# RWKV-7 mixer: a chunk's last doubling joins the first doubling of the next visit, and the products with the state take the array's full shape

## The chip, the cores and the metric

The kernel runs on one core of one Trainium2 chip. The metric is device time in microseconds of one execution, taken as the median of several runs. Beside them stands one execution under the hardware profiler, from which all rows below come.

## The reference

Two layers of a trunk over 1024 latent and 256 context tokens of width 1024, all in float32. Each layer: a modulated norm, one input projection, three groups of heads (gated linear attention, GLA; windowed softmax attention; RWKV-7), one output projection, and a SwiGLU feed-forward part. The change lies in the RWKV-7 scan, four heads of width 64 in two directions:

```python
def step(S, inp):
    rt, wt, kt, vt, kkt, at = inp
    sa = jnp.einsum('bhvk,bhk->bhv', S, kkt)
    S = (S * wt[:, :, None, :] - sa[..., None] * (kkt * at)[:, :, None, :]
         + vt[..., None] * kt[:, :, None, :])
    return S, jnp.einsum('bhvk,bhk->bhv', S, rt)
```

The kernel computes it in chunks of 64 tokens. Inside a chunk the sequential updates make a triangular system of 64x64 for each head and direction, so the kernel needs the inverse X of a unit triangular matrix. It finds it by doubling: the inverses of diagonal blocks of 2, 4, 8, 16 and 32 rows one after the other, and last the 64x64 one from its two blocks of 32. One doubling is two products with a copy between them: y = L·X of the smaller blocks, then w = X·y is put off the diagonal.

## The kernel before

The mixers of a layer run as generators, and a small planner (`Weave`) writes the order of TensorE's instructions by hand. It keeps a clock `TE.t` that each product advances by a planned cost, each generator yields the time it wants to wait before its next step, and of those whose time has come the one with the lowest rank goes first: `scan` (0), `prep` (1), `finish_all` (3), and last (9) the dense products of the input projection (`in_rest`, tile `ps_in`, 128x512 or 128x256), which therefore fill the gaps one by one. A generator can also wait for a mark, `yield after(("s", i - 3))`, until the planner has set it. One column of the projection is held back until the scans are done. The order of the other engines' instructions is the scheduler's, with those that go through `FIRST` preferred.

`prep` (line 1183) makes a visit for each of 20 chunks and one more. In visit i the younger chunk i gets its products with itself (`gram`, tile `ps_g`, 64-row shape, masked by VectorE into LQ), a first level on VectorE, and then the older chunk i-1 gets its own `ps_g` (into MP). Two steps follow in which both chunks double together: 64 products `ps_y` of the shape 32x32 (each float32 product is two instructions), ScalarE's copy y, 64 products `ps_w`, then on VectorE a predicated copy into X2 and a transpose into XT2. Chunk i goes through two doublings in visit i and two in visit i+1. At the end of visit i+1 stands the last doubling, of 32 to 64: 16 instructions into `ps_y6`, a copy, 16 into `ps_w6`, and copies into XF[p], which holds the four 32x32 blocks in 64 columns for each of the four matrices. Between them stand four transposes into `ps_kt`. Then the mark `("b", i - 1)` is set.

`scan` (line 1272) waits for that mark and for the scan before. It makes `ps_r` from two groups of eight full-shape products (MP with the values, AK with the state SBD), copies the result into R, multiplies it by X (128 rows, 64 columns, restarting the upper half of `ps_r`), copies that into VU and U, makes the new state with `ps_s`, sets `("s", i)`, and adds LQ·U (again 64 columns) to the lower half of `ps_r` for the output.

In the profile all products carry line 160 and all preferred instructions line 177, so tiles tell them apart; numbers at the end of a tile's name are left out, so `ps_y6` and `ps_w6` appear as `ps_y` and `ps_w` with 16 instructions.

Of the kernel before, what the change touches and what calls it, by code (L numbers as in the profile page):

```python
# [38 lines left out]
P = 128  # L39
# [106 lines left out]
def block_kernel(ctx: ExitStack, tc: tile.TileContext, a):  # L146
# [975 lines left out]
    def rwkv_mixer(l, t_first, pool, fpool, pp, spawn):  # L1122
# [23 lines left out]
        XF = [pool.tile([P, 4, 64], F32, name=f"XF{i}") for i in range(2)]  # L1146
# [36 lines left out]
        def prep():  # L1183
# [3 lines left out]
            for i in range(NC + 1):  # L1187
                yield after(("s", i - 3))
                p = i % 2
                young, old = batch[i] if i < NC else None, batch[i - 1] if i else None  # L1190
# [32 lines left out]
                for step in range(2):  # L1223
                    py = new([P, 2, 4, 32], "ps_y")
# [3 lines left out]
                    y = pool.tile([P, 2, 4, 32], F32, name="y", bufs=2)  # L1228
                    S.copy(y[:, hv], py[:, hv])
                    yield 1000  # L1230
                    pz = new([P, 2, 4, 32], "ps_w")
# [3 lines left out]
                    V.copy_predicated(f3(X2[:, hv]), lev2[:, step, p, hv].rearrange("p h n -> p (h n)"), f3(pz[:, hv]))  # L1235
                    V.transpose(f3(XT2[:, hv]), f3(X2[:, hv]))
                    yield 1200
                if old is None:
                    continue

                X, XT, LQ, xf = X2[:, 1 - p], XT2[:, 1 - p], old["LQ"], XF[p]
                for r in (0, 32, 64, 96):
                    (S.copy if r < 64 else G.tensor_copy)(xf[r:r + 32, :, r % 64:r % 64 + 32], X[r:r + 32])
                ab = [(h, v, d) for v in range(2) for d in range(2) for h in (0, 64)]
                py = new([P, 2, 32], "ps_y6")
                for h, v, d in ab:
                    ra, rb = (h, h + 32) if d == 0 else (h + 32, h)
                    TE.matmul(py[rb:rb + 32, v, :], LQ[ra:ra + 32, 2 * d + v, rb % 64:rb % 64 + 32],
                              XT[ra:ra + 32, 2 * d + v, :])
                y = pool.tile([P, 2, 32], F32, name="y6")  # L1250
                S.copy(y, py)
# [5 lines left out]
                yield 300  # L1257
                pz = new([P, 2, 32], "ps_w6")
                for h, v, d in ab:
                    ra, rb = (h, h + 32) if d == 0 else (h + 32, h)  # L1260
                    TE.matmul(pz[ra:ra + 32, v, :], y[rb:rb + 32, v, :], X[rb:rb + 32, 2 * d + v, :])
                for h in (0, 64):
                    for d in range(2):
                        ra, rb = (h, h + 32) if d == 0 else (h + 32, h)
                        (V.tensor_copy if d == 0 else S.copy)(
                            xf[ra:ra + 32, 2 * d:2 * d + 2, rb % 64:rb % 64 + 32], pz[ra:ra + 32])
                old["X"] = xf
                at["b", i - 1] = TE.t + 900
# [3 lines left out]
        def scan():  # L1272
            V, S, G = FIRST
            for i in range(NC):
# [19 lines left out]
                for u in range(4):  # L1294
                    TE.matmul(pr_[H[0], u, :], X[:, u, :], R[:, u, :], skip_group_check=True)
# [640 lines left out]
```

## Time and profile before

| | us |
|---|---|
| median of 3 runs | 3733.19 (3726.67 to 3733.74) |
| the profiled execution | 3721.78 |
| its span, first to last instruction | 3719.8 |
| TensorE busy, of the span | 3548.3 |
| VectorE, ScalarE, GpSimd busy | 2347.6, 1518.4, 693.1 |
| mean granted TensorE clock | 0.977 of full speed |

A row of the timeline gives the start of a group of like instructions, the time to the end of its last one, engine, line, operation, tiles, shape and count, and in brackets the idle time of the engine before it with what ended it. Products are pipelined: the end of a group overlaps the start of the next, so the time a group costs is read from its start to the start of the group behind it.

### The profile page before, as it was taken

How to read it: one execution, taken by the hardware profiler on the slowest of the kernel's cores; microseconds unless marked ns; L12 is line 12 of the kernel's file. 1: busy time of each engine (PE TensorE's matmuls, PEld its weight loads, DVE VectorE, ACT ScalarE, POOL GpSimd, SP SyncE). 2: the span in 40 equal slices, each digit the busy share in tenths (PEclk: the TensorE clock that was granted, in tenths of full speed). 3: DMA queues.
4: the chain of work that ended last, by engine and by line, in shares of the span. 5: the costliest groups of instructions: out<-in, count | busy, mean ns of one | idle time of the engine just before them, and what ended most of it. 6: DMA issues, size and time to landing. Idle time of an engine off the chain costs nothing. (4 is left out here: it accounts for less than half of the span.)

```text
span 3719.8 us, 76157 instructions
## 1 busy us (share of the span) xinstructions
PE 3548.3 (95%) x30714; PEld 2800.8 (75%) x30714; DVE 2347.6 (63%) x4516; ACT 1518.4 (41%) x3094; POOL 693.1 (19%) x979
## 2 busy tenths in 40 slices
PE   7988899999999999999999998989899999999998
PEld 4766778656788888888788766777777778888787
DVE  4764555556557777746776783455665676666766
ACT  4434543346324333333442543553366143333213
POOL 3122332111333000000341232232211340000002
PEclk8999999999999999999999999999989999999999
DMA  5253343553331333325421234343321332221611
GB/s 184 105 171 102 110 141 95 138 146 91 98 107 60 109 115 110 112 76 195 133 90 59 83 141 141 114 141 105 95 80 47 122 104 87 82 88 57 204 63 63
DMA packets 310768, 405.78 MB, mean 109 GB/s; under 512 B 52880, under 2 KB 210192, under 8 KB 308368
## 3 DMA queue, kind: packets, MB, share of 16 engines
q1 hardware_dynamic: 310416, 400.92, 34.3%
q8 instruction: 242, 3.96, 0.4%
q14 instruction: 110, 0.90, 0.1%
HBM read 290.54 MB, written 105.03 MB: 106 GB/s over the span
## 5 line engine op out<-in xcount | busy, mean ns | idle before, releaser
L160 PE MATMUL ps_in<-h,w_hl 128*128 128x512 f32 (+1 forms) x2928 | 708.1, 382 | 9.3 <-ACT w_hl L412 2.7
L160 PEld LDWEIGHTS ps_in<-h,w_hl 128*128 128x128 f32 x2928 | 486.6, 192 | 135.7 <-issue 52.1
L160 PE MATMUL ps_gu<-f,hl 128*128 128x512 f32 (+1 forms) x2400 | 566.4, 388 | 7.5 <-DVE hl L413 4.2
L160 PE MATMUL ps_d<-g,w_hl 128*128 128x512 f32 (+1 forms) x2688 | 556.2, 368 | 9.1 <-DVE x L1700 6.7
L160 PEld LDWEIGHTS ps_d<-g,w_hl 128*128 128x128 f32 x2688 | 462.9, 189 | 102.8 <-DVE x L1700 11.3
L160 PEld LDWEIGHTS ps_gu<-f,hl 128*128 128x128 f32 x2400 | 441.2, 189 | 102.2 <-DVE hl L413 5.1
L1700 DVE SCALAR_TENSOR_TENSOR x<-ps_d,mods,x 128x512 f32<-128x512 f32 (+1 forms) x448 | 291.0, 684 | 131.3 <-PE ps_d L160 130.7
L160 PE MATMUL ps_gu<-T,hl 128*128 128x512 f32 x1440 | 346.9, 390 | 1.5 <-DVE u L1601 1.5
L160 PEld LDWEIGHTS ps_gu<-T,hl 128*128 128x128 f32 x1440 | 268.8, 188 | 57.6 <-ACT g L412 1.9
L277 POOL TENSOR_TENSOR ada<-ada 128x256 f32<-128x256 f32 x112 | 89.2, 830 | 690.1 <-DMA x<-d_gt 557.2
L365 POOL TENSOR_TENSOR nacc<-nacc,nsq 128x512 f32<-128x512 f32 (+1 forms) x52 | 60.8, 1169 | 759.6 <-ACT nsq L364 744.6
L412 ACT CAST hl<-S 128x512 fp32r<-128x512 f32 x160 | 98.4, 620 | 249.4 <-PE ps_gu L160 155.8
L412 ACT CAST w_hl<-w_raw 128x1024 fp32r<-128x1024 f32 (+1 forms) x100 | 100.9, 1013 | 235.9 <-PE ps_d L160 199.3
L412 ACT CAST hl<-raw 128x512 fp32r<-128x512 f32 x156 | 96.6, 622 | 219.2 <-PE ps_gu L160 196.2
L1044 DVE TENSOR_REDUCE mx<-ps_ss 128x1 f32<-128x640 f32 (+2 forms) x144 | 107.5, 747 | 115.0 <-PE ps_ss L160 114.6
L160 PE MATMUL ps_o<-m,w_hl 128*128 128x512 f32 (+1 forms) x720 | 169.7, 383 | 0.0
L413 DVE TENSOR_TENSOR hl<-S,hl 128x512 fp32r<-128x512 f32 x160 | 110.0, 689 | 64.9 <-ACT hl L412 64.4
L160 PEld LDWEIGHTS ps_o<-m,w_hl 128*128 128x128 f32 x720 | 124.6, 191 | 31.0 <-issue 7.7
L413 DVE TENSOR_TENSOR w_hl<-w_raw,w_hl 128x1024 fp32r<-128x1024 f32 (+1 forms) x100 | 120.3, 1207 | 40.8 <-ACT w_hl L412 40.5
L413 DVE TENSOR_TENSOR pT<-ps_st,pT 128x512 fp32r<-128x512 f32 (+1 forms) x168 | 109.0, 657 | 33.4 <-ACT pT L412 32.9
L160 PEld LDWEIGHTS ps_x<-f,hl 128*128 128x128 f32 x960 | 124.5, 191 | 6.6 <-issue 0.8
L160 PE MATMUL ps_x<-f,hl 128*128 128x256 f32 x960 | 127.1, 283 | 0.0
(354 smaller groups left out, 5937.9 us busy)
## 6 DMA issues: line engine op xcount, KB each, us to landing
w_raw<-in_w_in_dram SPq DMA_DIRECT2D x44, 512.0 KB, 3.7
raw<-in_w_gate_dram SPq DMA_DIRECT2D x44, 512.0 KB, 3.5
raw<-in_w_up_dram SPq DMA_DIRECT2D x44, 512.0 KB, 3.7
x<-d_gt SPq DMA_DIRECT2D x88, 256.0 KB, 3.2
AK<-d_ab SPq DMA_DIRECT2D x80, 256.0 KB, 3.8
w_raw<-in_w_down_dram SPq DMA_DIRECT2D x40, 512.0 KB, 3.6
d_gt<-u SPq DMA_DIRECT2D x68, 256.0 KB, 2.2
d_ab<-W SPq DMA_DIRECT2D x16, 1024.0 KB, 3.9
```

What stands on the lines that cost most here:

```text
L160: return nc.tensor.matmul(out, lhsT, rhs, **kw)
L277: G.tensor_tensor(acc[:, s], acc[:, s], ps_[n % 2], ALU.add)
L365: (G if 0 < o < 5 else V).tensor_tensor(self.acc[g0], self.acc[g0], sq[:, :n], ALU.add)
L412: S.copy(dst[:, 0], src)
L413: V.tensor_tensor(dst[:, 1], src, dst[:, 0].bitcast(F32), ALU.subtract)
L1044: V.tensor_reduce(m_, psf[:, :nk * P], AX.X, ALU.max)
L1700: V.scalar_tensor_tensor(x[:, o, g0:g0 + n], ps[:, :n], mods[:, l, s, 40 + o:41 + o], x[:, o, g0:g0 + n], ALU.mult, ALU.add)
```

## The change

The visits become 22. The step "double both chunks" of a visit first takes, behind its own products, those of the last doubling of the chunk whose second doubling ended in the visit before; X and XT of that chunk are put into a tile XO for it, since X2 is taken over by the next young chunk. The mark "b" of a chunk is set there. XF is widened to 128 columns, with the right half zero, and holds X less the identity, so that X·R is added to R in `ps_r` in place of restarting it; LQ·U takes all 128 columns of LQ, and its upper half is not read. VU has two buffers in place of three.

```diff
-        XF = [pool.tile([P, 4, 64], F32, name=f"XF{i}") for i in range(2)]
+        XF = [pool.tile([P, 4, P], F32, name=f"XF{i}") for i in range(2)]
...
+            ab = [(h, v, d) for v in range(2) for d in range(2) for h in (0, 64)]
+            of = lambda h, d: (h, h + 32) if d == 0 else (h + 32, h)
+            last = None
-            for i in range(NC + 1):
+            for i in range(NC + 2):
                 yield after(("s", i - 3))
...
-                    old["VU"] = VU = pool.tile([P, 512], F32, name="VU", bufs=3)
+                    old["VU"] = VU = pool.tile([P, 512], F32, name="VU", bufs=2)
...
                     for h, LQ in both:
                         for u, rs, cs in blocks:
                             TE.matmul(py[rs, h, u, :], LQ[rs, u, cs], XT2[rs, h, u, :])
+                    if last is not None:
+                        py6, ob = new([P, 2, 32], "ps_y6"), last
+                        for h, v, d in ab:
+                            ra, rb = of(h, d)
+                            TE.matmul(py6[rb:rb + 32, v, :],
+                                      ob["LQ"][ra:ra + 32, 2 * d + v, rb % 64:rb % 64 + 32], XO[ra:ra + 32, 1, 2 * d + v])
+                    if both:
+                        y = pool.tile([P, 2, 4, 32], F32, name="y", bufs=2)
+                        S.copy(y[:, hv], py[:, hv])
+                    if last is not None:
+                        y6 = pool.tile([P, 2, 32], F32, name="y6")
+                        S.copy(y6, py6)
                     yield 1000
...
+                    if last is not None:
+                        pz6 = new([P, 2, 32], "ps_w6")
+                        for h, v, d in ab:
+                            ra, rb = of(h, d)
+                            TE.matmul(pz6[ra:ra + 32, v, :], y6[rb:rb + 32, v, :], XO[rb:rb + 32, 0, 2 * d + v])
...
+                    if last is not None:
+                        for h in (0, 64):
+                            for d in range(2):
+                                ra, rb = of(h, d)
+                                (V.tensor_copy if d == 0 else S.copy)(
+                                    last["X"][ra:ra + 32, 2 * d:2 * d + 2, rb % 64:rb % 64 + 32], pz6[ra:ra + 32])
+                        at["b", i - 2] = TE.t + 1200
+                        last = None
                     yield 1200
...
+                X, xf = X2[:, 1 - p], XF[p]
+                XO = pool.tile([P, 2, 4, 32], F32, name="XO")
+                S.copy(XO[:, 0], X)
+                S.copy(XO[:, 1], XT2[:, 1 - p])
+                last = old
+                old["X"] = xf
                 for r in (0, 32, 64, 96):
-                    (S.copy if r < 64 else G.tensor_copy)(xf[r:r + 32, :, r % 64:r % 64 + 32], X[r:r + 32])
+                    (V if r < 64 else G).tensor_tensor(
+                        xf[r:r + 32, :, r % 64:r % 64 + 32], X[r:r + 32],
+                        eye32[r:r + 32].unsqueeze(1).to_broadcast([32, 4, 32]), ALU.subtract)
...
                 for u in range(4):
-                    TE.matmul(pr_[H[0], u, :], X[:, u, :], R[:, u, :], skip_group_check=True)
+                    TE.matmul(pr_[:, u, :], X[:, u, :], R[:, u, :], start=False, stop=False, skip_group_check=True)
...
                 for u in range(4):
-                    TE.matmul(pr_[H[1], u, :], LQ[:, u, 64:128], U[:, u, :], start=False, stop=(u == 3),
+                    TE.matmul(pr_[:, u, :], LQ[:, u, :], U[:, u, :], start=False, stop=(u == 3),
                               skip_group_check=True)
```

The lines of the old last doubling at the visit's end (its `ps_y6`, copy, a wait of 300, `ps_w6`, copies, the mark) are taken out there; the four transposes into `ps_kt` stay.

## Rows read from the trace of the kernel before

**Rows 1.** The page, part 1: busy us, share of the span, instructions.
```profile
PE 3548.3 (95%) x30714; PEld 2800.8 (75%) x30714; DVE 2347.6 (63%) x4516; ACT 1518.4 (41%) x3094; POOL 693.1 (19%) x979
```
**Rows 2.** TensorE's waits, 275 to 690 us, then 2270 to 2680: us, times, longest.
```profile
PE ps_y L160 <- DVE XT L177: 10.8, 8, 2.7
PE ps_s L160 <- DVE VU L177: 4.9, 5, 1.0
...
PE ps_y L160 <- DVE XT L177: 9.5, 7, 3.5
PE ps_w L160 <- ACT y L177: 9.0, 9, 2.4
PE ps_r L160 <- ACT Rbd L177: 4.1, 5, 1.5
...
PE ps_y L160 <- DVE rw_rs_t L442: 1.8, 1, 1.8
```
**Rows 3.** Timeline of TensorE, one visit of the first layer (columns as told above).
```profile
640.88 1.66 PE L160 MATMUL ps_in<-h,w_hl 128*128 128x512 f32 x6
642.47 0.33 PE L160 MATMUL ps_y<-XT,LQ 32*32 32x32 f32 x16
642.73 0.66 PE L164 MATMUL ps_kt<-cst,Ke 128*128 128x128 f32 x4
643.14 0.71 PE L160 MATMUL ps_in<-h,w_hl 128*128 128x512 f32 x2
643.78 0.33 PE L160 MATMUL ps_w<-X,y 32*32 32x32 f32 x16
644.04 1.96 PE L160 MATMUL ps_g<-AK 64*64 64x128 f32 x32
...
646.73 1.05 PE L160 MATMUL ps_r<-Vbd,MP 128*128 128x128 f32 x8
647.62 1.06 PE L160 MATMUL ps_r<-SBD,AK 128*128 128x128 f32 x8
648.43 0.71 PE L160 MATMUL ps_in<-h,w_hl 128*128 128x512 f32 x2
...
654.68 1.09 PE L160 MATMUL ps_r<-Ubd,LQ 128*64 128x128 f32 x8
655.70 0.50 PE L160 MATMUL ps_in<-h,w_hl 128*128 128x512 f32 x1
```
**Rows 4.** Timeline of TensorE, the ends of both stretches.
```profile
687.32 7.89 PE L160 MATMUL ps_in<-h,w_hl 128*128 128x512 f32 x35
...
707.85 1.64 PE L160 MATMUL ps_in<-h,w_hl 128*128 128x512 f32 x6
...
2653.41 1.42 PE L160 MATMUL ps_in<-h,w_hl 128*128 128x512 f32 x5
...
2662.53 1.06 PE L160 MATMUL ps_r<-Rbd,XF 128*64 128x128 f32 x8 [0.62 <-ACT Rbd L177]
2663.52 0.45 PE L160 MATMUL ps_w<-X,y 32*32 32x32 f32 x32
2663.90 0.44 PE L164 MATMUL ps_f<-cst,fy 128*128 128x128 f32 x2
...
2673.49 1.06 PE L160 MATMUL ps_r<-Rbd,XF 128*64 128x128 f32 x8 [1.51 <-ACT Rbd L177]
2675.38 1.16 PE L160 MATMUL ps_s<-VU,KT 128*128 128x128 f32 x8 [0.83 <-DVE VU L177]
```
**Rows 5.** By tile: count, shortest/median/longest ns, first and last start in us, forms.
```profile
L160 PEld LDWEIGHTS ps_r<-SBD,AK x320: 192/192/333, 296.5 to 2671.4; 128*128 128x128 f32 x160
L160 PEld LDWEIGHTS ps_r<-Rbd,XF x320: 132/137/137, 299.7 to 2674.2; 128*64 128x64 f32 x160
L177 DVE TENSOR_TENSOR SBD<-ps_s,tmp x80: 374/422/429, 304.8 to 2677.1; 64x256 f32<-64x256 f32 x80
```
**Rows 6.** Timeline of TensorE at the longest wait for XT in the first layer.
```profile
443.59 0.33 PE L160 MATMUL ps_y<-XT,LQ 32*32 32x32 f32 x16 [2.69 <-DVE XT L177]
...
445.15 3.54 PE L160 MATMUL ps_g<-AK 64*64 64x128 f32 x32
```

More of the change, by code (lines that the diff above doesn't have):

```diff
@@ L1186, in prep @@
             load(0)
-            for i in range(NC + 1):
+            ab = [(h, v, d) for v in range(2) for d in range(2) for h in (0, 64)]
+            of = lambda h, d: (h, h + 32) if d == 0 else (h + 32, h)
+            last = None
+            for i in range(NC + 2):
                 yield after(("s", i - 3))
                 p = i % 2
-                young, old = batch[i] if i < NC else None, batch[i - 1] if i else None
+                young, old = batch[i] if i < NC else None, batch[i - 1] if 0 < i <= NC else None
                 hv = slice(0, 2) if i < NC and i else slice(p, p + 1) if old is None else slice(1 - p, 2 - p)
@@ L1223, in prep @@
                 for step in range(2):
-                    py = new([P, 2, 4, 32], "ps_y")
+                    if step and not both:
+                        break
+                    if both:
+                        py = new([P, 2, 4, 32], "ps_y")
                     for h, LQ in both:
@@ L1227, in prep @@
                             TE.matmul(py[rs, h, u, :], LQ[rs, u, cs], XT2[rs, h, u, :])
-                    y = pool.tile([P, 2, 4, 32], F32, name="y", bufs=2)
-                    S.copy(y[:, hv], py[:, hv])
+                    if last is not None:
[4 more added lines that the diff above has]
+                                      ob["LQ"][ra:ra + 32, 2 * d + v, rb % 64:rb % 64 + 32], XO[ra:ra + 32, 1, 2 * d + v])
+                    if both:
+                        y = pool.tile([P, 2, 4, 32], F32, name="y", bufs=2)
[3 more added lines that the diff above has]
+                        S.copy(y6, py6)
                     yield 1000
-                    pz = new([P, 2, 4, 32], "ps_w")
+                    if both:
+                        pz = new([P, 2, 4, 32], "ps_w")
                     for h, LQ in both:
@@ L1234, in prep @@
                             TE.matmul(pz[rs, h, u, :], y[rs, h, u, :], X2[rs, h, u, :])
-                    V.copy_predicated(f3(X2[:, hv]), lev2[:, step, p, hv].rearrange("p h n -> p (h n)"), f3(pz[:, hv]))
-                    V.transpose(f3(XT2[:, hv]), f3(X2[:, hv]))
+                    if last is not None:
[3 more added lines that the diff above has]
+                            TE.matmul(pz6[ra:ra + 32, v, :], y6[rb:rb + 32, v, :], XO[rb:rb + 32, 0, 2 * d + v])
+                    if both:
+                        V.copy_predicated(f3(X2[:, hv]), lev2[:, step, p, hv].rearrange("p h n -> p (h n)"),
+                                          f3(pz[:, hv]))
+                        V.transpose(f3(XT2[:, hv]), f3(X2[:, hv]))
+                    if last is not None:
[6 more added lines that the diff above has]
+                        last = None
                     yield 1200
@@ L1239, in prep @@
                     continue
-                X, XT, LQ, xf = X2[:, 1 - p], XT2[:, 1 - p], old["LQ"], XF[p]
-                for r in (0, 32, 64, 96):
-                    (S.copy if r < 64 else G.tensor_copy)(xf[r:r + 32, :, r % 64:r % 64 + 32], X[r:r + 32])
[L1244 to L1251, printed above, removed]
+                X, xf = X2[:, 1 - p], XF[p]
[4 more added lines that the diff above has]
+                old["X"] = xf
+                for r in (0, 32, 64, 96):
+                    (V if r < 64 else G).tensor_tensor(
+                        xf[r:r + 32, :, r % 64:r % 64 + 32], X[r:r + 32],
+                        eye32[r:r + 32].unsqueeze(1).to_broadcast([32, 4, 32]), ALU.subtract)
                 pt = new([P, 4, P], "ps_kt")
@@ L1256, in prep @@
                 S.copy(KT, pt)
[L1257 to L1268, printed above, removed]
         ow = fpool.tile([P, NT, 256], F32, name="ow")
```

## The prediction, made before the changed kernel was seen

> **What bounds the kernel now.** I read the page first: TensorE is busy for 95% of the span [rows 1], so TensorE's own queue ends last nearly everywhere, and a change is worth the TensorE time it takes away plus the TensorE waits it removes. The edit touches only the two stretches in which the RWKV visits run (about 256 to 687 us in the first layer, 2253 to 2677 us in the second). So next, who kept TensorE waiting inside them: most of it is XT (VectorE's transpose after a doubling) and y (ScalarE's copy between the two products of a doubling); R and VU, copies inside the scan, cost less. The six entries of [rows 2] hold 40 us of waits in 40 visits. Third, TensorE's timeline of a visit that has no wait at all [rows 3]: it shows the order that the planner wrote, products of the chain (ps_y, ps_w, ps_g, ps_r) with dense products (ps_in) in every gap. Here TensorE is full, and what costs is the seams: where the shape of the products changes, the next group starts later than the work before it takes. Last, the ends of the two stretches, where the dense work runs out [rows 4].
>
> **The change, part by part.**
>
> **1. The last doubling's own two groups go.** Before, a visit ends with 16 small products (ps_y x16), the transposes ps_kt, two dense products and 16 more (ps_w x16). From [rows 3]: six dense products and the step into the 32-row shape take 640.88 to 642.47, 1.59 us. A dense product takes 0.22 (34 intervals in 7.89 us less the last one's 0.4, at 687.32 [rows 4]), so six are 1.32 and the seam is 0.27. The 16 products until ps_kt: 0.26. Two dense until ps_w: 0.64, the seam 0.20. The 16 until ps_g: 0.26. Together 0.99 us. After, these 32 products stand right behind the products of the two younger chunks' first doubling, in the same shape. 32 of them take 0.38 until the next shape (2663.52 to 2663.90 [rows 4]) where 16 take 0.26, so 32 more cost between 0.24 (by that slope) and 0.38: I take 0.31. ps_g must then pay a seam of its own, 0.14 to 0.20. Saved: 0.99 - 0.31 - 0.17, about 0.5 us a chunk (0.4 to 0.6).
>
> **2. Full shape for X·R and LQ·U.** Eight full-shape products go on to another full-shape group after 0.89 us (646.73 to 647.62) and to a dense product after 0.81 (647.62 to 648.43) [rows 3]. The narrow LQ·U takes 1.02 until the dense product behind it (654.68 to 655.70): 0.21 saved there, and the seam between ps_s and LQ·U goes too, bounded by 0 and 0.2; I take 0.1. X·R has the same two seams where its neighbours are dense and none to save where they are 32-row groups: 0 to 0.3, I take 0.15. Nothing is added to the products: 192 ns of weight load for a full-shape product against 137 for a narrow one [rows 5], but eight full-shape pairs pass in 0.89 us, so the load lies under the products. Parts 1 and 2 give 0.5 + 0.31 + 0.15 = 0.95 us a chunk, bounds 0.6 and 1.1. Two layers have 40 chunks: **-38 us** (-24 to -44).
>
> Here the Trainium skill speaks against the change: its page "TensorE: Matmul & The Clock Gate", section "The mechanism" (Part 3), says that a weight load overlaps running products only when it goes to another row group. By that the wider load would stand in the open; it is the fourth rival below.
>
> **3. The waits at a visit's end go.** Before, ps_y x16 needs the X and XT that the second doubling has just made, and VectorE is often late with them behind rope, GLA and normalisation work. Of the 20.3 us of waits for XT [rows 2] all but 2.0 stand before a group of 16; the longest is 2.69 us at 443.59 [rows 6]; another 3.0 us is put down to VectorE's rw_rs, such as the 1.8 [rows 2]. Of the waits for y, eight with 5.4 us stand before ps_w x16. After, ScalarE copies X and XT off into XO, and the product that reads XO comes a whole front of a visit later (two ps_g and at least 3.4 us planned): 18.3 + 3.0 + 5.4 = **-27 us**. After the longest stall ps_g took 3.54 us for what takes 1.96 elsewhere ([rows 6], [rows 3]), TensorE at the lower of its two clocks: a few such cases less, **-3 us**. Where the stalls go is the first rival.
>
> **4. New work on the other engines.** A visit loses two ScalarE and two GpSimd copies into XF, and gains two ScalarE copies into XO, two VectorE and two GpSimd subtractions. A subtraction of 32x128 lies between nothing and the 0.42 us of a 64x256 sum [rows 5]. What hides them is the front of the next visit; VectorE is 63% and ScalarE 41% busy [rows 1]. I cost them at zero; without that cover VectorE's two are up to 0.8 us a visit, 34 us. On ScalarE and VectorE the copy of y6 and the four copies into X are moved from behind the second doubling to behind the next visit's first one, so that visit's y, copy and transpose are ahead of them, and the second doubling's are queued behind the copies; X·R, which needs them, comes after the eight products of two ps_r groups, so they have some 3 us. VU has two buffers instead of three: a load into it waits for the ps_s of two chunks before, which is done when a visit starts, so SP's queue does not stand behind it. No DMA is added or moved.
>
> **5. The chain gets longer and the order changes.** This is the price. Before, chunk i was ready at the end of visit i+1, and that visit waited for scan i-2: visits and scans ran side by side. After, chunk i is ready in the first step of visit i+2, that visit waits for scan i-1, and scan i waits for that visit: the front of a visit and a scan are one chain. The planner's own figures in the code set the order (not the time). Before, a visit adds up to 15.3 by them (ps_g 1.84, wait 3.4, four groups 4.34 and their waits 4.4, the end 1.3), and the scan's products, which go first, push it to some 17. After, the chain is ps_g 1.84, 3.4, the first doubling with the old one's last 1.36 + 1.0 + 1.36, 1.2, ps_r 1.72, 1.2, X·R 0.86, 1.5, ps_s 0.86, 1.1, together 17.4, and the second doubling squeezed in pushes it to some 18.5. So about 1 us more of dense work, five products, is laid into each visit. It is not unlimited. In the first layer 105 dense products (four rows, the first and the last in [rows 4]) follow the last scan, of which the column that is held back takes 72: 33 are left over. In the second none is, the last stands at 2653.41 [rows 4]. Five more in 20 visits: dense work runs out some 2 visits earlier in the first layer and 3 in the second. What a visit without dense work costs shows the second layer's end: five waits, 0.62 the first, 1.51 the longest, 0.83 the last [rows 4], 4.1 us together. I take 3 us for each of five visits: **+15 us** (+6 to +25). And X·R has now always one group between itself and ps_r, which is what it had at 2662.53 (half such a group), with 0.62 us in the open [rows 4]. I take 0.25 a chunk: **+10 us** (+4 to +20).
>
> **The sum.** -38 - 27 - 3 + 15 + 10 = -43 us. The profiled execution took 3721.78 us (its span 3719.8), so the like of it would take 3679. The runs' median, 3733.19, lies 11.4 us above that execution, and I carry that over: 3690 us. All the best bounds: -44 - 27 - 8 + 6 + 4 = -69; all the worst, with half of the waits back: -24 - 14 + 25 + 20 = +7.
>
> **The rivals.**
> (a) *The stalls come back.* VectorE is late because of what else is in its queue, not because of where the chain asks for it, and 25 of the 30 us reappear at R, VU and the first doubling. Then -43 + 25 = -18, 3715 us. For it: VU and R are waited for already, 9 us [rows 2]. Against it: between a doubling's copy and its next use now lie two whole ps_r groups.
> (b) *The serial chain decides* (slower). R, VU and U are now on a chain that nothing runs beside. If each scan pays what the second layer's last one paid, 1.51 for R and 0.83 for VU [rows 4], and 1.0 for U like the longest wait for VU [rows 2], that is 3.3 us a chunk and 134 us, less some 15 that these waits cost today: -68 + 119 = +51, 3784 us. It turns the result to slower once these waits pass 68 / 40 = 1.7 us a chunk above today's. Against it: the gaps planned ahead of ps_s and LQ·U are as long as before, only that ahead of X·R shrinks. Part of its price, +10 to +30, is likelier than all of it.
> (c) *No difference.* Dry visits and the waits for R at their upper bounds (45 us) against shape and waits at two thirds of theirs: within 7 us of before.
> (d) *The wider load is open.* 55 ns more for each [rows 5], 16 loads a chunk, 40 chunks: +35, so -8 us, 3725. The row speaks against it: eight full-shape loads and products pass in 0.89 us [rows 3], and 1.54 us of loads alone would not fit.
> By the page's rule those eight would stand one behind the other; the trace does not agree.
>
> **How the numbers follow.** Forecast (-25 to -70 us) 0.55; (a) 0.20; (b) 0.12; (c) 0.10; (d) 0.03. A measurement can tell about 0.2%, 7.5 us, from no change. Faster: 0.55 + 0.20 + 0.02 = 0.77; same 0.10 + 0.01 = 0.11; slower 0.12. The range goes from about the best bound over (a), (c) and (d) to a small (b) and leaves the rest out: 3655 to 3738.
>
> **What would show it.** Right: no ps_y or ps_w group of 16 but groups of 80 that take some 0.85 us; LQ·U followed by a dense product after 0.81; hardly a wait for XT; dense products that end two or three visits before the scans do. Wrong: more than 1.7 us a visit of waits for R, VU and U; the lower clock in the dry visits; a gain or a loss in another stage, which I take as unchanged.

## The result: slower, and the profile of the changed kernel

The changed kernel takes 3756.43 us (median of 4 runs, 3754.33 to 3765.0) against 3732.01 us before (4 runs, 3726.67 to 3733.74). The ratio is 1.0071, 95% interval 1.0053 to 1.009: slower by 0.7%, where 1.2% faster was forecast.

The page of the profiled execution, part 1, and the line with the core's span and mean granted clock (before: [rows 1], span 3719.8 us, clock 0.977):

```profile
PE 3547.9 (95%) x30714; PEld 2834.6 (76%) x30714; DVE 2367.6 (63%) x4596; ACT 1514.2 (40%) x3094; POOL 700.3 (19%) x979
core 0: 3752.6 us, clock 0.967
```

TensorE is busy for as long as before, 3547.9 and 3548.3 us, and that hides two opposite movements. The span falls into three parts: idle time (span less busy), time lost to the clock (span times the missing share of the clock) and the rest, work as if at full clock.

| us | before | after | difference |
|---|---|---|---|
| idle | 3719.8 - 3548.3 = 171.5 | 3752.6 - 3547.9 = 204.7 | +33 |
| lost to the clock | 3719.8 x 0.023 = 86 | 3752.6 x 0.033 = 124 | +38 |
| work at full clock | 3463 | 3424 | -39 |

It is an estimate, good to some 10 us: the clock has three digits (2 us either way), a wait in a stretch of lower clock counts in two parts, and the two halves of the change, run alone below (e1 and e2), come out at -19 and -33 by the same sum, more together than the -39 of both. The profiled execution of the kernel before is also one of its better ones: in its 25 runs beside e5 the mean granted clock is 0.974, which makes 96 us in place of 86, and the four runs of the changed kernel have 0.966, 129 us. So some 33 of the 38 us of clock are the kernel's. But it says where to look: the work shrank by about what parts 1 and 2 of the prediction forecast (-38), and idle time and clock took nearly twice that away.

Next, where. The two chunk stages are cut into visits 2 to 14 (counted from 0) and visits 15 to the end. The view of busy time in stretches, of the kernel before, then of after; columns: length, busy us of PE, PEld, DVE, ACT and POOL with their instructions, granted clock, DMA share, GB/s:

```profile
292.93:568.02 275.09, 247.68 (x5201) 196.89 (x5192) 138.82 (x321) 140.40 (x338) 80.58 (x136) 0.99 0.40 120
568.02:687.20 119.18, 116.47 (x2328) 96.45 (x2320) 70.65 (x254) 44.51 (x122) 29.28 (x51) 1.00 0.34 95
2287.82:2563.88 276.06, 253.30 (x5180) 201.88 (x5170) 133.62 (x270) 138.99 (x330) 78.30 (x135) 0.97 0.41 121
2563.88:2677.60 113.72, 105.93 (x2256) 86.14 (x2248) 65.90 (x249) 42.54 (x118) 29.01 (x51) 1.00 0.26 74
```
```profile
289.27:594.55 305.28, 275.62 (x5375) 232.64 (x5374) 153.03 (x355) 148.59 (x354) 84.82 (x137) 0.97 0.42 122
594.55:707.10 112.55, 93.87 (x2207) 83.59 (x2206) 67.42 (x263) 37.99 (x112) 28.69 (x51) 0.89 0.25 69
2309.50:2610.57 301.07, 277.07 (x5323) 229.92 (x5322) 146.78 (x300) 145.72 (x342) 82.88 (x133) 0.96 0.40 118
2610.57:2711.00 100.43, 78.46 (x2130) 70.63 (x2129) 64.59 (x258) 33.84 (x105) 28.41 (x51) 0.90 0.25 68
```

Idle is the length less the first busy time. In visits 2 to 14 it was 27.4 + 22.8 = 50.2 us and is 53.7: no better. At the ends it was 2.7 + 7.8 = 10.5 and is 18.7 + 22.0 = 40.7, and the clock there, 1.00 before, is 0.89 and 0.90, another 22 us. So 52 us of the loss sits in the visits from 15 on.

TensorE's timeline shows why. First visit 16 of the first layer, the last with dense work, then visits 17 and 18, which have none (dry visits, from here on):

```profile
614.06 1.96 PE L160 MATMUL ps_g<-AK 64*64 64x128 f32 x32
615.96 3.93 PE L160 MATMUL ps_in<-h,w_hl 128*128 128x512 f32 x16
619.81 0.72 PE L160 MATMUL ps_y<-XT,LQ 32*32 32x32 f32 x62
...
620.37 0.33 PE L160 MATMUL ps_y<-XO,LQ 32*32 32x32 f32 x14
620.63 1.42 PE L160 MATMUL ps_in<-h,w_hl 128*128 128x512 f32 x5
...
630.54 1.06 PE L160 MATMUL ps_r<-Ubd,LQ 128*128 128x128 f32 x8
631.44 0.60 PE L164 MATMUL ps_kt<-cst,Ke 128*128 128x128 f32 x4
631.97 1.96 PE L160 MATMUL ps_g<-AK 64*64 64x128 f32 x32
638.48 0.92 PE L160 MATMUL ps_y<-XT,LQ 32*32 32x32 f32 x53 [4.55 <-DVE XT L177]
...
649.00 1.96 PE L160 MATMUL ps_g<-AK 64*64 64x128 f32 x32
654.27 0.71 PE L160 MATMUL ps_y<-XT,LQ 32*32 32x32 f32 x62 [3.30 <-DVE rw_rs_y L439]
655.62 0.86 PE L160 MATMUL ps_w<-X,y 32*32 32x32 f32 x48 [0.48 <-ACT y L177]
657.68 0.28 PE L160 MATMUL ps_w<-X,y 32*32 32x32 f32 x4 [1.19 <-issue]
658.10 2.08 PE L160 MATMUL ps_r<-Vbd,MP 128*128 128x128 f32 x8
659.97 1.91 PE L160 MATMUL ps_r<-SBD,AK 128*128 128x128 f32 x8
```

The edit itself is as forecast: ps_y of 80 passes in 0.82 us (619.81 to 620.63), and the full-shape LQ·U in 0.90 (630.54 to 631.44). But the gap behind ps_g, which 16 dense products fill in the first visit shown, is empty from 631.97 on: TensorE stands for 4.55 and 3.30 us until VectorE and ScalarE have made XT from ps_g's result. VectorE in the first of the two, then the start of LQ in the second:

```profile
633.01 0.80 DVE L177 TENSOR_TENSOR XF<-X,c_eye 32x128 f32<-32x128 f32 x1
633.84 0.88 DVE L177 TENSOR_TENSOR SBD<-ps_s,tmp 64x256 f32<-64x256 f32 x2
634.75 0.87 DVE L177 TENSOR_TENSOR ow<-ps_r,ow 64x256 f32<-64x256 f32 x2
635.64 0.69 DVE L177 TENSOR_TENSOR LQ<-ps_g,c_mgr 128x512 f32<-128x512 f32 x1
...
638.02 0.31 DVE L177 STREAM_TRANSPOSE XT<-X 128x128 f32<-128x128 f32 x1
...
651.37 0.69 DVE L177 TENSOR_TENSOR LQ<-ps_g,c_mgr 128x512 f32<-128x512 f32 x1
```

In the first the scan's sums and the new subtraction into XF stand ahead of LQ, which starts at 635.64, when TensorE has been idle since 633.93; from LQ to the end of XT it is another 2.7 us (635.64 to 638.33). In the second LQ starts 0.4 us after the end of ps_g (649.00 + 1.96), so nearly the whole wait is the way from LQ to XT itself; rw_rs_y (normalisation), to which the profile puts it down, only runs in between on VectorE. Behind such a wait eight full-shape products take 1.87 us (658.10 to 659.97) instead of 0.89 [rows 3]: the lower of the two clocks (over the visit the granted clock is 0.81). By the counts of ps_in in each visit, visits 2 to 14 now take 44 dense products each in the first layer and 40 in the second (31 and 29 before). So the first layer has none from visit 17 on, and the second has four from visit 15 on.

### The profile page after: what moved, and what is told of

The parts are those of the page before. It is cut to its first block, busy times and chain, and to the rows that moved or that the text cites. A ratio compares the mean times of both kernels' runs of the same rounds, so it can differ in the third digit from the quotient of the medians.

```text
span 3752.6 us, 76286 instructions
## 1 busy us (share of the span) xinstructions
PE 3547.9 (95%) x30714; PEld 2834.6 (76%) x30714; DVE 2367.6 (63%) x4596; ACT 1514.2 (40%) x3094; POOL 700.3 (19%) x979
## 3 DMA queue, kind: packets, MB, share of 16 engines
q1 hardware_dynamic: 310416, 400.92, 34.1%
## 5 line engine op out<-in xcount | busy, mean ns | idle before, releaser
L160 PE MATMUL ps_in<-h,w_hl 128*128 128x512 f32 (+1 forms) x2928 | 683.4, 380 | 10.2 <-ACT w_hl L412 3.1
```

Source lines behind the costliest of these rows:

```text
L160: return nc.tensor.matmul(out, lhsT, rhs, **kw)
```

## The experiments

By the planner's own clock (`TE.t`; it sets the order, not the time) a visit lasts 17.4 us before and about 20.0 in the changed kernel (17.6 where no dense product is left); the prediction's 18.5 had been added up by hand. Three theories were put to the test. **A**: visits planned longer take more dense products, those run out, and the dry visits behind them carry the loss. **B**: the wider weight loads of the full shape stand in the open. **C**: VectorE and ScalarE are late with R, VU, y and XT in the visits that also have rope and GLA, so that a wait removed in one place comes back in another. This table sums up each kernel's profile, by the same stretches as above; the ratio is to the kernel before on the same chip. The profile columns are of one execution each, which can lie some way from the median of its kernel (e9's 14 us above, e2's 9 above, e12's 8 below).

| kernel | median us | ratio, 95% interval | dense a visit, visits 2 to 14 | idle, visits 2 to 14 | idle, ends | lost to the clock, both |
|---|---|---|---|---|---|---|
| before | 3732 to 3736 | | 31, 29 | 50.2 | 10.5 | 11 + 0 |
| after | 3756.43 | 1.0071, 1.0053 to 1.009 | 44, 40 | 53.7 | 40.7 | 21 + 22 |
| e1 full shape alone | 3726.59 | 0.9977, 0.9965 to 0.9988 | 31, 29 | 52.8 | 11.9 | 25 + 5 |
| e2 move alone | 3759.69 | 1.0065, 1.004 to 1.0091 | 44, 40 | 50.6 | 34.9 | 18 + 20 |
| e3 after, least share 300 | 3745.17 | 1.0027, 1.0013 to 1.004 | 36, 33 | 64.7 | 15.5 | 29 + 4 |
| e5 and front wait 2300 | 3731.87 | 1.0, 0.9986 to 1.0014 | 30, 27 | 64.6 | 14.1 | 25 + 6 |
| e6 e1, front wait 5500 | 3816.24 | 1.0228, 1.0208 to 1.0247 | 42, 38 | 68.7 | 60.5 | 32 + 39 |
| e4 after, two columns held back | 3767.87 | 1.0088, 1.0071 to 1.0105 | 44, 37 | 64.0 | 43.9 | 27 + 25 |
| e4b before, two held back | 3747.67 | 1.004, 1.0019 to 1.006 | 31, 29 | 49.1 | 20.5 | 14 + 9 |
| e14 after, none held back | 3768.91 | 1.01, 1.0083 to 1.0117 | 44, 40 | 55.0 | 26.9 | 28 + 21 |
| e7 after, fronts filled | 3761.1 | 1.008, 1.0058 to 1.0102 | 44, 40 | 52.9 | 25.0 | 27 + 13 |
| e9 behind the front | 3726.47 | 0.9986, 0.9971 to 1.0001 | 31, 28 | 46.9 | 13.3 | 27 + 5 |
| e10 e9, share 300 | 3725.11 | 0.9983, 0.9974 to 0.9993 | 24, 21 | 52.3 | 21.9 | 15 + 7 |
| e11 e10, ps_w later | 3712.74 | 0.9935, 0.9916 to 0.9954 | 30, 26 | 50.0 | 7.0 | 16 + 0 |
| e12 e10, y6 before ld | 3729.48 | 0.9985, 0.9971 to 0.9999 | 24, 21 | 51.1 | 16.3 | 18 + 8 |

**e1 and e2: one half of the change each.** The kernel before with the full shape:

```diff
-                    (S.copy if r < 64 else G.tensor_copy)(xf[r:r + 32, :, r % 64:r % 64 + 32], X[r:r + 32])
+                    (V if r < 64 else G).tensor_tensor(
+                        xf[r:r + 32, :, r % 64:r % 64 + 32], X[r:r + 32],
+                        eye32[r:r + 32].unsqueeze(1).to_broadcast([32, 4, 32]), ALU.subtract)
...
-                    TE.matmul(pr_[H[0], u, :], X[:, u, :], R[:, u, :], skip_group_check=True)
+                    TE.matmul(pr_[:, u, :], X[:, u, :], R[:, u, :], start=False, stop=False, skip_group_check=True)
...
-                    TE.matmul(pr_[H[1], u, :], LQ[:, u, 64:128], U[:, u, :], start=False, stop=(u == 3),
+                    TE.matmul(pr_[:, u, :], LQ[:, u, :], U[:, u, :], start=False, stop=(u == 3),
```

> The full shape alone: the last doubling stays at the end of its visit as before; XF is 128 wide and holds X less the identity, X·R and LQ·U take all 128 columns. Theory A (dense products spent too early: the new chain makes the planner lay 44 dense products into a visit in place of 32, they run out 4 and 6 visits before the scans end, and the dry visits idle 4 to 5 us each at a lower clock): the shape is a gain of its own, 0.3 to 0.6 us a chunk, 12 to 24 us less than the kernel before, about 3714 us. Theory B (the wider weight loads are not hidden): 0 to 35 us more than before, 3732 to 3767. Theory C (VectorE and ScalarE late in the visits that have rope and GLA beside them, whatever the dense work): like A here, a little less for the two VectorE subtractions, 3715 to 3730.

3726.59 us, 0.2% faster: C's range, where A had said about 3714. B falls: the wider loads cost nothing, in the trace LQ·U goes on to a dense product after 0.81 us (583.21 to 584.02), as the prediction had it. The work at full clock falls by 19 us (3463 to 3444), part 2's 40 x 0.46 = 18. Two thirds of that don't arrive. In the profiled execution the lower clock takes some 26 us more than before, of which about 10 lie far behind both stages, where the edit changes nothing; but that is for the most part the pair of executions. Over its 12 runs e1 has a mean granted clock of 0.973, the 23 runs of the kernel before beside it 0.974: 6 us more. With 4 us more of idle time (175.1 against 171.5) that makes -19 + 4 + 6 = -9, where the medians show -6.

e2 is the reverse of this diff on the changed kernel: the move with narrow products.

> The moved doubling alone: as in the changed kernel, but X·R and LQ·U in 64 columns, XF 64 wide, X itself and not X less the identity. Theory A: the whole loss is here, and without the shape's gain it is larger: 3756 + 12 to 24, about 3774 us, with the same 44 dense products a visit and the same dry visits at the end. Theory B: close to the kernel before or faster, 3700 to 3735. Theory C: 3756 to 3775, with the long waits for y and VU in visits 3 to 10.

3759.69 us, again C's range and 14 below A's. All of the loss is in the move; with or without full shape the same visits run dry. What the full shape is worth on top of the move isn't shown: the intervals of e2 and after overlap.

**e3 and e5: the changed kernel with a shorter planned visit.** The planner gives the dense products the first turn while they had less than `SHARE` of its last 3400 ns. e3:

```diff
-SHARE = (1000, 1000)
+SHARE = (300, 300)
```

> The changed kernel with one number changed: the planner's least share of dense work, 1000 in every 3400 of its own time, is 300. The planner's own period of a visit falls from 20.0 to 18.3, so 9 or 10 dense products fewer stand in a visit. Theory A: dense work lasts 2 to 3 visits longer in each layer, at 5 to 6 us saved for each, 22 to 34 us less than the changed kernel: 3722 to 3734 us, and a clock near 1.00 in more of the last 100 us of the stretches. Theory C: the long waits in visits 3 to 10 stay, with less dense work to cover them: 3750 to 3765.

e5, with e3's edit:

```diff
-                yield 3400 if young is not None else 0
+                yield 2300 if young is not None else 0
```

> The changed kernel with a least share of dense work of 300 (was 1000) and a front wait of 2300 (was 3400) in the planner: by the planner's own clock a visit then lasts 17.2 us as in the kernel before (17.4), not 20.0, so the dense products last to the end of both stages. Theory A (the dense products are spent early and the visits behind them run dry): the dry end's extra idle time (18 us in L0, 13 in L1) and the lower clock there (12 and 10) go, and about 3756 - 40 = 3715 us is left (3705 to 3725). Theory C (in every visit the longer chain through the last doubling leaves less room for VectorE and ScalarE, which still have rope and GLA): the waits of visits 2 to 13 rise as the visits get shorter, by 1 to 2 us a visit, and the whole comes to 3735 to 3755.

With a planned visit of 20.0, 18.3 and 17.2 us the time is 3756, 3745 and 3732, both times between the forecasts of A and C. The ends behave as A says: their idle time falls from 40.7 to 15.5 and 14.1. But the visits 2 to 14 give 11 us of that back, in the waits that C names. TensorE's waits in the first stage, 275 to 690 us, of after and then of e5; columns: us in total, times, longest:

```profile
PE ps_w L160 <- ACT y L177: 11.1, 7, 4.6
PE ps_y L160 <- DVE XT L177: 9.3, 5, 4.6
PE ps_s L160 <- DVE VU L177: 7.8, 4, 4.2
PE ps_r L160 <- ACT Rbd L177: 2.3, 4, 1.7
```
```profile
PE ps_y L160 <- DVE XT L177: 9.9, 7, 2.0
PE ps_r L160 <- ACT Rbd L177: 9.4, 9, 2.6
PE ps_y L160 <- ACT gl_u L714: 6.3, 2, 3.5
PE ps_s L160 <- DVE VU L177: 3.9, 3, 1.4
```

y and VU get better, R (2.3 to 9.4) and GLA's own gl_u come up. Both theories hold, A for the 25 us that come back, C for why it is not more than 25.

What makes the copies late can be read from the other engines. In the changed kernel the longest wait for y, 4.59 us, ends at 421.17. ScalarE, then VectorE, just before:

```profile
420.13 0.62 ACT L663 CAST qk_hl<-in 128x512 fp32r<-128x512 f32 x1 [8.18 <-issue]
420.66 0.37 ACT L177 COPY y<-ps_y 128x256 f32<-128x256 f32 x1
```
```profile
417.52 0.69 DVE L660 TENSOR_TENSOR t<-t,rope 128x512 f32<-128x512 f32 x1 [4.82 <-DMA t<-in]
419.36 0.69 DVE L661 TENSOR_TENSOR in<-in,t 128x512 f32<-128x512 f32 x1 [1.16 <-POOL in L657]
```

ScalarE isn't busy: it does nothing for 8.18 us, though ps_y has been done since 414.9, and copies y right behind rope's cast, whose input VectorE makes at 419.36, after standing 4.82 us for a load of rope's input. The two longest waits for VU, 4.16 us at 460.89 and 3.54 at 2476.17, have the same shape: VectorE stands 4.91 and 2.77 us for that load, and VU's copy runs behind rope's operations. These waits of VectorE over the whole span, before and then after (us, times, longest):

```profile
DVE t L660 <- DMA t<-in: 11.9, 7, 3.4
```
```profile
DVE t L660 <- DMA t<-in: 33.6, 12, 4.9
```

They are 34.8 us in e2 and 35.4 in e3, but 17.1 in e5 and 8.3 in e11. So part of C is an order of instructions that makes a ready copy stand behind a load. Why VectorE waits longer for this load in the changed kernel, and what an order without it would give, no run tested.

**e6: a long visit without the move.** e1's kernel, whose last doubling stands where it stood before, with a longer wait behind the front:

```diff
-                yield 3400 if young is not None else 0
+                yield 5500 if young is not None else 0
```

> The kernel before with the full shape alone (3726.6 us, a visit of 17.4 us by the planner's clock), and the wait behind a visit's front products set to 5500 in the planner (was 3400): a visit is then 19.7 us by the planner's clock, as in the changed kernel (20.0), and takes as many more dense products, while the last doubling stays where it was in the kernel before. Theory A (it is the planned length of a visit, hence the dense products that it takes and the dry visits behind them, that costs): the dense products run out some 3 visits before each end and the time is 3726.6 + 20 to 27 = 3746 to 3754 us. Theory C (it is the last doubling as a link of the chain, whatever a visit's planned length): 3722 to 3732.

3816.24 us, 90 more than e1: A's direction, at over three times its price, and far from C's "whatever its planned length". The ends of e6, in stretches:

```profile
610.29:731.80 121.51, 95.83 (x2169) 82.75 (x2160) 68.57 (x262) 33.95 (x99) 30.21 (x51) 0.86 0.21 61
2648.11:2769.60 121.49, 86.71 (x2099) 76.33 (x2094) 63.44 (x255) 30.58 (x92) 29.25 (x51) 0.82 0.18 49
```

25.7 and 34.8 us idle at 0.86 and 0.82 of the clock. Its dry visits last about 20 us, those of the changed kernel 14 to 18. So as far as these two orders go, the move makes a visit without dense work shorter, not longer; but the kernel before hardly had such visits. In visits 2 to 14 idle time rises too, from 52.8 to 68.7, so the forced length costs there as well, which A had not counted.

**e4, e4b, e14: fewer or more dense products for the visits.** `HOLD` is the number of columns of the projection that are held back until the scans are done. e4 is the changed kernel, e4b the kernel before, both with

```diff
-HOLD = 1
+HOLD = 2
```

> The changed kernel with the suspected cost made larger: two columns of the projection are held back until the scans are done in place of one, so 72 dense products fewer a layer lie beside the visits and run after them at full rate. Theory A: 1.6 visits more of each layer are dry, at 5 to 6 us each: 16 to 20 us more than the changed kernel, about 3774 us. Theory C: the same products only move, 3752 to 3760.

> The kernel before with two column tiles of the SSM projection held back to the end (was one), so that its chunk stage has some 30 dense products fewer; the same edit in the changed kernel cost 11 us. Theory A (a dry visit is dear in the changed order because its chain is longer): here it costs clearly less, 0 to 5 us. Theory C (dry visits cost the same in both orders, the loss lies in the visits with rope and GLA): 9 to 13 us.

e4 costs 11 us over after by the medians, between the two forecasts (the intervals of the two ratios overlap, so this is weak), e4b 15 us over before, more than either. In e4b only the second layer gets two more dry visits, and its end goes from 7.8 us of idle to 16. My reason in A for why a dry visit would be dearer in the changed order, its longer chain, falls; e6 says the same. e14 goes the other way:

```diff
-HOLD = 1
+HOLD = 0
```

> The changed kernel with no column tile of the SSM projection held back (was one): some 30 dense products more can be spent among the visits of each stage. Theory A (the dry visits at the ends of the stages carry the loss): one dry visit fewer in L0 and in L1, each worth 4 to 5 us of idle time and 1.7 to 3.5 us of clock, so 3756 - 10 to - 16 = 3740 to 3746 us. Theory C (the waits in the visits with rope and GLA carry it): 3752 to 3760 us, as those visits stay as they are.

3768.91 us: worse by 12 by the medians, and both forecasts missed. The dry ends do shrink, from 40.7 to 26.9 us of idle, but there is no dense product left behind the last scan, and TensorE waits there for what it normally has cover for; its waits over the whole span:

```profile
PE ps_f L164 <- DVE fy L1356: 17.3, 4, 7.9
```

The dense products are one fixed stock: what a stage spends early is missing at its end, and what it does not hold back is missing behind it. This run does not separate A from C.

**e7: the fronts of dry visits filled.** The changed kernel with three throw-away products in the front of the last visits; the output does not use them:

```diff
+                if i >= (17, 15)[l] and young is not None:
+                    junk = sg.tile([P, 512], F32, name="ps_junk", tag="d", bufs=2)
+                    for _ in range(3):
+                        nc.tensor.matmul(junk, eye, old["AK"][:, 0:2].rearrange("p u w n -> p (u w n)"))
```

> The changed kernel with three throw-away products of 128 x 512 (0.27 us each at full clock or so) put into the front of each visit from the 17th of L0 and the 15th of L1 on, where the dense products have run out; the work is more by 4 + 6 visits of about 0.8 us, in time that was idle before ps_g's result. If the lower granted clock of the dry visits (22 us lost there) follows from TensorE's idle time in them: 3756 - 8 to - 15 = 3741 to 3748. If it does not: 3754 to 3762.

3761.1 us, by the intervals not to be told from after, and in the range for a clock that does not follow from the idle time. But the expectation mis-sized its own edit: the three run as six instructions and take 2.84 us a visit instead of 0.8, some 23 us in eight visits. So some 23 us of work were added for no time that can be measured: idle time at the ends falls from 40.7 to 25.0 and the clock's loss there from 22 to 13. Idle time and the lower clock go together here; that the one causes the other is likely, but this run does not show it alone, since three of the five filled visits of the second layer still ran at 0.82 to 0.90.

**e9 to e12: the last doubling behind the front.** Full shape as in the change, but the old chunk's last doubling (the products and copies of the change, taken out of the first doubling) stands right behind ps_g of the next visit, in the gap that a dry visit leaves empty, with groups of its own:

```diff
-                yield 3400 if young is not None else 0
+                if last is not None:
+                    py6, ob = new([P, 2, 32], "ps_y6"), last
...
+                    y6 = pool.tile([P, 2, 32], F32, name="y6")
+                    S.copy(y6, py6)
+                    yield 1000
+                    pz6 = new([P, 2, 32], "ps_w6")
...
+                    at["b", i - 2] = TE.t
+                    last = None
+                    yield 2100 if young is not None else 0
```

> Full shape as in the changed kernel, but the last doubling of the old chunk stands right behind the front products (ps_g) of the next visit, not with the first doubling of the younger chunks: its two groups are separate again (about 0.5 us a chunk more than in the changed kernel), they fill the wait for XT after ps_g, and the old chunk's state steps can start one third of a visit earlier; by the planner's clock a visit lasts 17.4 us as before. Theory A (the loss is the longer chain of a visit and the dense products it takes): no dry end, tail waits gone, about the time of the full shape alone (3726.6) less 5 to 27 us: 3700 to 3722. Theory C: the late waits of R, U and VU stay and it comes to 3722 to 3740.

3726.47 us, 30 less than after, with the planned visit back at 17.4: no dry end, 13.3 us of idle in it. But it is not faster than e1, nor clearly faster than e5, which has a like planned visit and the step in its old group, and it lies in C's range; a new wait has come, that for y before ps_w. e10 lowers `SHARE` to 300 (some 16 us a visit):

> As e9_behind_front, with the planner's least share of dense work at 300: a visit is 15.9 us by the planner's clock (17.4 there), so fewer dense products stand between the steps of a visit. Theory A alone would let the time fall with the planned length as it did from 20.0 (3756) over 18.3 (3745) to 17.2 us (3732), some 8 us for each us: 3712 to 3718. Theory C (below the length of the kernel before, the waits for R, U, VU and y in the visits with rope and GLA grow by what is taken away): 3724 to 3735.

3725.11 us, C's range: the visits get shorter and the waits eat it. One wait stands out, ahead of the last doubling's second group. ScalarE, then TensorE, in one visit of e10:

```profile
455.41 1.22 ACT L177 COPY ld<-LQ 32x128 f32<-32x128 f32 x4 [0.38 <-DVE LQ L177]
456.65 0.21 ACT L177 COPY y<-ps_y 128x64 f32<-128x64 f32 x1
```
```profile
453.01 0.33 PE L160 MATMUL ps_y<-XO,LQ 32*32 32x32 f32 x16
453.26 1.45 PE L160 MATMUL ps_in<-h,w_hl 128*128 128x512 f32 x5
456.91 0.33 PE L160 MATMUL ps_w<-XO,y 32*32 32x32 f32 x16 [2.20 <-ACT y L177]
```

ps_y is done at 453.34, but its copy is queued behind the four ld copies, which wait for LQ; TensorE stands 2.20 us. e11 puts dense products into that gap, e12 puts the group and its copy (as a function, y6_of_last) ahead of the ld copies:

```diff
 e11:
-                    yield 1000
+                    yield 2000
-                    yield 2100 if young is not None else 0
+                    yield 1600 if young is not None else 0
 e12:
                     gram(young["AK"], 3, LQ)
+                    y6_of_last()
                     ld = pool.tile([P, 4, 32], F32, name="ld")
```

> As e10_short_visit, with the wait between the two groups of the last doubling at 2000 in the planner (was 1000) and that behind it at 1600 (was 2100): 16.8 us a visit. In e10 TensorE waits 33.2 us in 25 waits for y before ps_w, most of it for the y6 copy, which stands on ScalarE behind the four ld copies. Theory A': dense products put into that gap cover the wait, and the waits that are left do not grow: 3725 - 15 to - 25 = 3700 to 3710 us. Theory C (what is taken from one wait comes back in the next link, R, U or VU, as ScalarE and VectorE set the pace in the visits with rope and GLA): 3718 to 3728.

> As e10_short_visit, with the first group of the last doubling between the two products of the front, so that the y6 copy stands ahead of the ld copies on ScalarE instead of behind them; the planned visit stays 15.9 us. Theory A': the wait for y6 (most of 33.2 us in 25 waits before ps_w in e10) goes: 3725 - 20 to - 30 = 3695 to 3705 us. Theory C (it comes back at R, U, VU or XT): 3715 to 3728.

e11 takes 3712.74 us, 0.65% faster than the kernel before (0.46 to 0.84%), 44 us faster than the changed one and 19 faster than e5 by the medians: the best of all kernels here, between the forecasts of A' and C. That wait over the whole span, in e10 and in e11:

```profile
PE ps_w L160 <- ACT y L177: 33.2, 25, 4.0
```
```profile
PE ps_w L160 <- ACT y L177: 3.3, 7, 1.0
```

and e11's stretches:

```profile
291.02:555.98 264.96, 240.17 (x5172) 200.57 (x5171) 143.91 (x341) 139.33 (x333) 81.28 (x134) 0.97 0.41 119
555.98:674.60 118.62, 113.83 (x2336) 96.84 (x2336) 77.74 (x269) 45.86 (x128) 35.54 (x56) 1.00 0.37 106
2282.05:2545.48 263.43, 238.18 (x5120) 196.38 (x5119) 138.19 (x292) 136.10 (x325) 78.23 (x134) 0.97 0.42 122
2545.48:2660.20 114.72, 112.52 (x2330) 95.88 (x2330) 72.74 (x262) 45.20 (x125) 31.39 (x52) 1.00 0.31 86
```

The ends have 4.8 + 2.2 = 7.0 us of idle at full clock. In visits 2 to 14 the idle time is what it was before (50.0); there C holds: R's waits, 21.7 us in e10, are 25.3 here. But of the 30 us taken from the one wait only a part came back: idle time over the whole span is 168.5 us, 12 less than in e10. How much of e11's gain over e1 (14 us) is the moved doubling and how much its shorter planned visit and lower `SHARE` is open: full shape alone was not run with those. e12, 3729.48 us (0.9985, 0.9971 to 0.9999), takes 8.8 instead of 33.2 us of that wait and has the waits for XO (6.4) and KT (6.1) in its place; its narrow group also cuts ps_g's in two. Within 0.2% of before, and inside neither forecast.

## Why the prediction was wrong

The forecast was -43 us, the measurement +24. Two terms failed. Part 3 counted waits as gone that came back at the next copies (-30 forecast, no gain measured), and part 5 sized the dry visits at +15 where they cost 52.

**Parts 1 and 2, the work (-38).** Right as far as the estimate goes: -39 by the sum of the result, and the rows that were to show it do: 0.82 us for a ps_y of 80 ("some 0.85"), groups of 16 only in the last visit, LQ·U on to a dense product after 0.81 in e1. The fourth rival, the wider load, is shown wrong by e1. The rule of the Trainium skill that stood for it (page "TensorE: Matmul & The Clock Gate", section "The mechanism", Part 3: a weight load overlaps running products only in another row group) doesn't agree with that run either; the same section's opening also lets a load into the background weight buffer go ahead, and that the prediction left out.

**Part 3, the waits at a visit's end (-27, and -3 of clock).** Wrong. The idle time of visits 2 to 14 went from 50.2 to 53.7 us, the clock's loss from 11 to 21 (some 5 us of the clock's whole loss are the two executions, as above). The waits were read rightly, but for one: 2.69 us is the longest of the first layer only, the second has 3.5 [rows 2]. The waits for XT before the groups of 16 are gone. By the timelines of visits 2 to 14 the waits for XT fell from 18.8 to 9.0 us, those for VU rose from 5.4 to 15.1, R's from 2.4 to 4.9, and y's stayed (10.9 and 11.2, with one of 4.6 now the longest). This is rival (a), in full. The step that failed is "where a stall goes": XO's consumer was moved a front later, but y, R and VU of the same visit stayed on the same two queues, behind the same rope and GLA; what is read under e5 shows it for three of the longest waits. e3, e5 and e10 show such an exchange too.

**Part 4, the new work (0).** Right where dense work lies beside it: e1, which has the subtractions, has 52.8 us of idle time in visits 2 to 14 against 50.2. Two VU buffers, not run alone, seem to cost little: SP's queue waited 28.3 us before and 34.1 after at VU's loads, in both stretches together, so the prediction's "does not stand behind it" holds only as a difference. In the dry visits the cover that the step named is gone, and XF's 0.80 us stands ahead of LQ in the rows above; that is part of the next term.

**Part 5, the dry visits (+15).** The mechanism was right, the size was the error. The planned visit is 20.0 us, not 18.5: the forced least share of dense work also lies in the chain, which I had added up without it (with a share of 300 it is 18.3). A visit therefore takes 12 more dense products, not five. Four visits in the first layer and six in the second run dry, not two and three more. Each costs not 3 us but the idle time and the clock: +30 and +22 us at the ends, 52 where 15 was put down and 25 was its upper bound. The lower clock in dry visits stood in the prediction only among what would make it wrong, without a price. The one dry end that I had priced from [rows 4] ran at full clock.

**Part 5, the waits for R (+10), and rival (b).** Half of it: R has 10.0 us in 12 waits over the whole span (4.8 in 7 before), +5.2, within the bounds. VU has 18.1 (6.2 before), and U's 3.9 are gone, so the three together rose by some 13 us, 0.3 a chunk. They are part of the idle time counted above and below. The serial chain decides, but through the dense products that it uses up, not through R, VU and U, and rival (b)'s 1.7 us a visit was never reached. The slower outcome came from a term of the sum that was capped too low, not from the mechanism that carried the chance of slower.

**Sum.** Forecast -38 - 30 + 15 + 10 = -43. Measured in the profiled executions: work -39; visits 2 to 14 +3.5 of idle and +10 of clock; ends +30 and +22; the rest of the program +6; together +33, the difference of the spans (3752.6 - 3719.8), and +24 in the medians. The two differ mostly because the profiled execution before was 10 us faster than its kernel's median.

**What stays open.** The lost clock is a sum over stretches, and which waits cost clock and which don't was not settled. e1's lower clock in visits 2 to 14 (25 us lost against 11, with 52.8 us of idle time against 50.2) is one execution against another; the means of the runs leave 6 us of it over the whole span. Waits put down to "issue" such as the 1.19 us at 657.68 have no cause that a run shows. And e6's price, three times what A said, isn't explained by A.

## What to carry to other kernels

Filler work is a stock: before a chain of dependent steps is made longer, count how much filler each of its steps will take by the planner's own numbers (run it, don't add it up by hand), and what the last steps cost when the filler is gone, clock included. A step that is moved off one wait may be better put into a gap than into a group that the chain waits for: at a planned visit of some 17 us e11 does the one and is 19 us faster than e5, which does the other; e9 was not clearly so. And a wait on an engine that is late because of its queue is often not removed by asking elsewhere: most of it reappears at the next thing that this engine makes. So look at what stands ahead in that queue, and whether the engine is busy there or waits itself.

## What the runs showed of the hardware that was not expected

- Packing and full shape gave what had been priced: 80 products of 32x32 in 0.82 us, and eight full-shape products with the wider loads until the dense product behind them in 0.81 us (e1), the narrow ones in 1.02 [rows 3].
- Idle time at TensorE cost more than half as much again in clock in the dry stretches (22 us with 40.7, 39 with 60.5), but not at one price: visits 2 to 14 lost 11 to 32 us with 47 to 69 us of idle time. The ends of the stages kept a granted clock of 1.00 with 7 to 10.5 us of waits (e11, before), had 0.89 and 0.90 with 40.7, and 0.86 and 0.82 with 60.5 (e6). A dry stretch is to be priced with both.
- Work put into a wait can be nearly free: in e7 some 23 us of throw-away products lengthened the program by no more than the measurement can tell (1.008 of the kernel before, against 1.0071).
- An engine that others wait for can be idle itself: ScalarE did nothing for 8.18 us ahead of the copy that TensorE waited for (e5's section), since rope's cast stood first and its input was late.
